# A pool mixer on rounded parts: three float32r products instead of one 32-bit product

## The chip, the cores and the metric

The kernel runs on one core of a Trainium2 chip. Times are device microseconds (us) of one launch. The median of three runs of the kernel before is 1588.48 us (1587.77 to 1590.91).

The core has five engines with a queue each: PE (TensorE, matrix products), DVE (VectorE), ACT (ScalarE), POOL (GpSimd) and SP (SyncE, which issues most DMA transfers). Each engine works through its queue in order, and waits on counters that other engines and transfers raise.

## The reference

Three layers over 512 tokens of 1024 features: a pool mixer with a feed-forward, latent attention with a feed-forward, differential attention with a routed mixture of 16 experts. Only the first step is changed, the pool mixer of layer 0 (its 1024 features are in four groups of 256, with windows of 2, 4, 8 and 16 tokens):

```python
def pool_mixer(h, w, scale):                 # h = rms_norm(x) * gain
    hf = h.reshape(B, S, 4, 256)
    cs = cumsum(hf, axis=1)
    for g, win in enumerate((2, 4, 8, 16)):
        c = cs[:, :, g]
        lag = pad(c[:, :-win], ((0, 0), (win, 0), (0, 0)))
        mean = (c - lag) / minimum(n_avail, win)[:, None]
        outs.append(mean - hf[:, :, g])      # a band matrix over tokens, less the identity
    y = einsum('bsgc,gcd->bsgd', stack(outs, axis=2), w)
    return y.reshape(B, S, D) * scale        # x = x + y
```

## The kernel before

The features lie on the 128 partitions, so x is eight tiles `x[:, d]` of 128 features by 512 tokens. `pool_mixer` computes the weight product first and the band after it, since both are linear and the norm's factor is one number per token:

1. `gains` (DVE): the group's weights `pw` times the norm's gain, two halves of 128x256.
2. `squares` (ACT, DVE): the square of each tile of x, added up on DVE; then `col_sums` (PE, a product with `ones` into the bank `pst`), `rcolv` (DVE) and the power -1/2 (POOL) give `rcol`, one factor per token.
3. `products` (PE): per group and pair of token tiles, x as the stationary operand against `pw`, into one PSUM bank; eight banks in all (four tagged `acc`, two `pss`, two `pst`). The products of groups 2 and 3 stand behind the column sums in PE's queue.
4. `evac`: each bank times `rcol` into a tile `z`, its first half by ACT and its second half by DVE.
5. the band products (PE): per feature tile, five products of `z` with the band matrix `bnd`, into an `acc` bank.
6. `finish`: DVE adds the scaled bank to x; ACT and DVE split the new x times the next gain into two float32r parts `xh` and `xl` (`xh` on ACT is the rounded value, `xl` on DVE the rest); ACT squares it and POOL adds the squares into `ss` for the norm of the feed-forward.

The products of `gains`, `products` and the bands are plain 32-bit ones; the profile shows each as two records. Everything later works on split operands: `mm3` makes three float32r products (high by high, high by low, low by high) of one.

Beside this the task `weights` starts the split of the feed-forward's first weights: a chunk `raw` of 128x2048 comes by DMA, ACT rounds a 128x512 part of it to `hi`, and DVE or POOL (parts 2 and 4) writes the rest to `lo`.

The order of instructions on each engine is fixed at build time. `Sched` interleaves the tasks: the ready task of the lowest rank goes next, and `Plan` keeps a rough line of time for each engine to say when a tile is ready. In this plan a chunk of weights counts as present. `gains` and `weights` have rank 0, `squares` and `evac` 1, `products` 2. All operations are issued in one wrapper, so the profile names them all L341. The feed-forward that follows needs all eight `xh` and `xl` in its first product, and the column sums of `ss` stand behind that product in PE's queue.

Of the kernel before, what the change touches and what calls it, by code (L numbers as in the profile page):

```python
# [17 lines left out]
P = 128  # L18
# [16 lines left out]
# the stream of the experts' weights: pieces in the arena while attending, routing, in the experts;  # L35
# pieces split ahead; chunks in the room of parts before the rows are gathered; chunks that come
# in pieces
# [4 lines left out]
# which parts of a chunk Pool takes the second halves of (feed-forward and first attention; second)  # L42
# [39 lines left out]
class Stream:  # L82
    """Weights in the order of their use: loaded ahead, split into two float32r parts ahead.
    Some are loaded into the arena, and the room of those that are not can take their parts.
    The experts' (from item `first` on) are split and used 512 columns at a time; they are
    loaded into the arena, up to `ahead` such pieces, or where parts had been."""
# [23 lines left out]
    def load(self):  # L110
        """as many of the coming ones as there is room for"""
# [59 lines left out]
    def open(self, t):  # L171
        """the first load after `hold`, and so all that follow, wait for the gathers before it"""
        if self.gate:
            self.net.nc.gpsimd.memset(t[:, :1], 0.0)
            self.gate = False

    def room(self):
        """the tags that the parts of the next one to split can have, if any are free"""
# [65 lines left out]
    def gone(self, i, last):  # L244
        """a part of item i is split"""
# [11 lines left out]
    def pump(self, n=1):  # L257
        """n more parts of the splits, as far as there is room"""
# [19 lines left out]
    def release(self, w=None):  # L278
        """the last use of w (or of the longest held) is issued"""
        i = 0 if w is None else [h is w for h, _ in self.held].index(True)  # L280
        for tag in self.held.pop(i)[1]:
            self.spare[tag] += 1
        if self.split >= self.first:
            self.load()
# [16 lines left out]
    def piece(self):  # L301
        """the next 512 columns of the experts' weights"""
# [7 lines left out]
class Plan:  # L310
    """What is issued, on each engine's line of time by a rough price list: when a tile will
    be there, so that a piece that needs it is issued no earlier."""
# [43 lines left out]
    def dma(self, price, *outs):  # L356
        """a transfer (into `outs`)"""
# [40 lines left out]
class Sched:  # L398
    """Interleaves tasks (generators) in program order. A task yields a tile that its next
    piece needs, or how long to wait; the first ready task of the lowest rank goes next."""  # L400
# [31 lines left out]
class Direct:  # L432
    """The weights of one expert whose number is known at run time only."""
# [20 lines left out]
class Net:  # L454
# [21 lines left out]
    def get(self, tag, n=1):  # L476
        """n PSUM banks, when as many are free"""
# [6 lines left out]
    def put(self, tag, n=1):  # L484
        """the last use of n banks is issued"""
# [18 lines left out]
    def hilo(self, hi, lo, src):  # L504
        """hi + lo = src"""
# [3 lines left out]
    def split(self, hi, lo, src, g=None):  # L509
        """hi + lo = src, or src * g, as a task"""  # L510
# [10 lines left out]
    def hilo_g(self, hi, lo, src, g):  # L521
        """hi + lo = src * g, g one number per partition"""
# [40 lines left out]
    def square_sum(self, key, src, first, scale=1.0, eng=None):  # L563
        """adds src^2 (one feature tile) to the sum of the norm"""
# [9 lines left out]
    def col_sums(self, key, ps=None):  # L574
        """sums of the squares per token, [token of the tile, tile], in PSUM"""
# [17 lines left out]
    def bcast(self, col, name, ps=None):  # L593
        """[token of the tile, tile] -> [every partition, token]"""
# [10 lines left out]
    def new_norm(self, gname, keep=False):  # L605
        """the parts of the coming norm's x; the ones in use stay with who holds the lists"""
# [4 lines left out]
    def prep(self, d, eng=None):  # L611
        """the split of x * gain, and the sum of squares, of feature tile d"""
# [4 lines left out]
    def norm_hooks(self):  # L617
        """what the first products of a phase leave to the tensor engine in between"""
# [8 lines left out]
    def pool_mixer(self):  # L627
        """tasks"""
        nc, a, sched = self.nc, self.a, self.sched
        self.ss = {}  # L630
        pw, bands, zs = [], [], {}
        for g in range(4):
# [7 lines left out]
        for g in range(4):  # L640
            b = self.tmp("bnd")
            nc.sync.dma_start(out=b[:, :384], in_=a["bands"][:, g])
            nc.dma(0.55, b)
            bands.append(b)
# [5 lines left out]
        def gains(g):  # L650
            yield pw[g]
            for k in range(2):
                c = slice(k * 256, (k + 1) * 256)
                nc.vector.tensor_scalar(pw[g][:, c], pw[g][:, c], self.vec("mix0", 2 * g + k),
                                        None, op0=OP.mult)

        def squares():
            for d in range(KT):
                yield self.x[:, d]
# [17 lines left out]
        def evac(g, jj, tag, ps):  # L677
# [3 lines left out]
            z = self.tmp("z")  # L681
            for j in range(2):
                o = slice(j * 256, (j + 1) * 256)
                r = self.rcol[:, 2 * jj + j:2 * jj + j + 1]
                if j:
# [1512 lines left out]
```

## Time and profile before

| what | value |
|---|---|
| median of three runs | 1588.48 us |
| span of the profiled execution, first to last instruction | 1588.0 us |
| own time of the profiled execution beside its span | not given; the median is 0.48 us above the span |
| PE busy | 1525.1 us, 96% |
| DVE, ACT, POOL busy | 1016.4, 773.0, 504.2 us |
| pool mixer, start to the first product of the feed-forward | 37.2 us |
| column sums of the feed-forward's norm on PE | from 44.73 us |

A row of the timeline gives the start, the time taken, the engine, and what is written from what; in brackets how long the engine sat idle before it and what ended the wait. Several equal instructions in a row are merged, with their count. A window's row gives its length, then the busy time (and count) of PE, PE's weight loads, DVE, ACT and POOL, PE's granted clock (1.00 is full speed, 2.4 GHz, and 0.50 is 1.2 GHz), the DMA engines' busy share and the GB/s moved. PE records are pipelined: the time from one start to the next is the price, not the length of one.

### The profile page before, as it was taken

To read this page: it belongs to the slowest core of one execution; us is meant where nothing else is said; L and a number is where in the kernel's file an instruction comes from. 1 tells how busy PE (TensorE), PEld (TensorE's weight loads), DVE (VectorE), ACT (ScalarE), POOL (GpSimd) and SP (SyncE) were. 2 spreads that over 40 slices of the span, in tenths; PEclk is the share of its full clock that TensorE was granted. 3 is DMA by queue.
4 is the path that set the end of the run, shared out by engine and by line. 5 is a ranking of instruction groups with operands and counts; after the bars stand their busy time and mean duration, and the time that the engine had idled before them with its cause. 6 is when DMAs were issued, how large, how long until landed. Compare 5 with 4: busy or idle time off the path is not lost. (4 is left out here: it accounts for less than half of the span.)

```text
span 1588.0 us, 21545 instructions
## 1 busy us (share of the span) xinstructions
PE 1525.1 (96%) x7752; PEld 1238.5 (78%) x7752; DVE 1016.4 (64%) x1668; ACT 773.0 (49%) x1569; POOL 504.2 (32%) x382
## 2 busy tenths in 40 slices
PE   7999999999999999999999999999999699999996
PEld 6788888888878788888888889889868566666664
DVE  5564344445477755443444467887884599999996
ACT  5323222323366633232223345566672378787875
POOL 3322122312241113221223123312221465565653
PEclk9999999999999999999999999999989699999998
DMA  6131323223210223213222232111067889999961
GB/s 237 61 106 55 118 106 106 89 74 103 83 44 29 65 107 119 98 58 123 106 107 71 84 124 81 54 54 67 27 205 260 243 305 357 371 350 352 341 209 29
DMA packets 69934, 221.60 MB, mean 140 GB/s; under 512 B 7616, under 2 KB 16960, under 8 KB 56640
## 3 DMA queue, kind: packets, MB, share of 16 engines
q1 hardware_dynamic: 56448, 201.03, 35.4%
q0 software_dynamic: 4064, 14.16, 3.8%
q10 hardware_dynamic: 9312, 5.01, 1.1%
q8 instruction: 62, 1.02, 0.3%
q14 instruction: 48, 0.39, 0.1%
HBM read 208.63 MB, written 11.53 MB: 139 GB/s over the span
## 5 line engine op out<-in xcount | busy, mean ns | idle before, releaser
L341 POOL TENSOR_TENSOR lo<-raw,hi 128x512 fp32r<-128x512 f32 (+1 forms) x157 | 224.4, 1440 | 714.1 <-ACT hi L341 625.8
L341 PE MATMUL acc<-xh,hi 128*128 128x512 f32 x744 | 290.5, 390 | 0.5 <-ACT xh L341 0.5
L341 PE MATMUL acc<-xl,hi 128*128 128x512 f32 x744 | 289.6, 389 | 0.3 <-DVE xl L341 0.3
L341 PE MATMUL acc<-xh,lo 128*128 128x512 f32 x744 | 289.5, 389 | 0.0
L341 DVE TENSOR_TENSOR wl<-raw,wh 128x512 fp32r<-128x512 f32 x288 | 264.8, 970 | 9.1 <-ACT wh L341 8.8
L341 ACT ACTIVATE hi<-raw 128x512 fp32r<-128x512 f32 (+1 forms) x378 | 208.7, 607 | 86.4 <-issue 59.8
L341 DVE TENSOR_TENSOR lo<-raw,hi 128x512 fp32r<-128x512 f32 (+1 forms) x221 | 211.7, 968 | 19.8 <-ACT hi L341 19.0
L341 ACT ACTIVATE wh<-raw 128x512 fp32r<-128x512 f32 x384 | 212.4, 621 | 16.2 <-PE acc L341 10.4
L341 POOL TENSOR_TENSOR wl<-raw,wh 128x512 fp32r<-128x512 f32 x96 | 143.3, 1493 | 123.8 <-ACT wh L341 88.8
L341 PEld LDWEIGHTS acc<-xh,hi 128*128 128x128 f32 x744 | 139.7, 188 | 29.6 <-ACT xh L341 1.0
L341 PEld LDWEIGHTS acc<-xl,hi 128*128 128x128 f32 x744 | 139.7, 188 | 29.3 <-DVE xl L341 0.6
L341 PEld LDWEIGHTS acc<-xh,lo 128*128 128x128 f32 x744 | 139.6, 188 | 29.1
L341 DVE TENSOR_TENSOR u<-acc,R 128x512 f32<-128x512 f32 x44 | 30.4, 691 | 181.1 <-PE acc L341 181.1
L341 PE MATMUL acc<-hh,hi 128*128 128x512 f32 x352 | 136.9, 389 | 0.0
L341 PE MATMUL acc<-hl,hi 128*128 128x512 f32 x352 | 136.9, 389 | 0.0
L341 PE MATMUL acc<-hh,lo 128*128 128x512 f32 x352 | 136.9, 389 | 0.0
L341 ACT ACTIVATE hh<-t 128x512 fp32r<-128x512 f32 x44 | 27.8, 632 | 218.4 <-DVE t L341 218.4
L341 DVE TENSOR_TENSOR x<-acc,x 128x512 f32<-128x512 f32 x59 | 40.5, 689 | 124.2 <-PE acc L341 124.2
L341 PE MATMUL acc<-hi,xh 128*128 128x256 f32 x384 | 112.7, 293 | 0.0
L341 PE MATMUL acc<-lo,xh 128*128 128x256 f32 x384 | 108.6, 283 | 0.0
L341 PE MATMUL acc<-hi,xl 128*128 128x256 f32 x384 | 108.5, 283 | 0.0
L341 PE MATMUL acc<-wh,teh 128*96 128x512 f32 x256 | 106.7, 417 | 0.0
(308 smaller groups left out, 2915.4 us busy)
## 6 DMA issues: line engine op xcount, KB each, us to landing
raw<-moe_w SPq DMA_DIRECT2D x200, 256.0 KB, 6.6
raw<-moe_w SPq DMA_DIRECT2D x46, 1024.0 KB, 8.4
raw<-ffn_gu SPq DMA_DIRECT2D x43, 1024.0 KB, 4.8
raw<-ffn_dn SPq DMA_DIRECT2D x32, 704.0 KB, 4.1
raw<-da_in SPq DMA_DIRECT2D x12, 1024.0 KB, 4.9
raw<-mla_up SPq DMA_DIRECT2D x4, 832.0 KB, 4.4
raw<-mla_o_a SPq DMA_DIRECT2D x12, 256.0 KB, 4.3
raw<-da_o_a SPq DMA_DIRECT2D x12, 256.0 KB, 4.2
```

What stands on the lines that cost most here:

```text
L341: r = f(*args, **kw)
```

## The change

x, the weights and z are split in two float32r parts, the weights' product becomes three products by `mm3`, and the bands become products of both parts of z with a rounded band. The band matrix is laid out anew on the host: four pieces of 128x512 whose first 128 columns are cut to their high bits, and a fifth piece with what the cut left; before it was four pieces of 128x384. New tasks are `parts` (rank 0: the split of x, high on ACT, low on DVE) and `rounded` (rank 0: POOL copies the bands to float32r). `gains` splits the weights, `evac` the bank: both halves on ACT (`zh`) and again on DVE (`zl`). `squares` now starts once a tile's parts are issued.

```diff
+        for g in range(5):
+            t = self.tmp("bndr")
+            nc.sync.dma_start(out=t, in_=a["bands"][:, g])
...
         def gains(g):
+            h = self.pair("pw")
             for k in range(2):
                 c = slice(k * 256, (k + 1) * 256)
-                nc.vector.tensor_scalar(pw[g][:, c], pw[g][:, c], self.vec("mix0", 2 * g + k),
-                                        None, op0=OP.mult)
+                self.hilo_g(h[0][:, c], h[1][:, c], pw[g][:, c], self.vec("mix0", 2 * g + k))
...
+        def rounded():
+            for t in raws:
+                yield t
+                b = self.tmp("bnd", F32R)
+                nc.gpsimd.tensor_copy(b, t)
+                yield b
+                bands.append(b)
+
+        def parts():
+            for d in range(KT):
+                yield self.x[:, d]
+                h = self.pair("xp")
+                self.hilo(*h, self.x[:, d])
+                xs[d] = h
 
         def squares():
             for d in range(KT):
-                yield self.x[:, d]
+                while xs[d] is None:
+                    yield 0.1
...
-                if j:
-                    nc.vector.tensor_scalar(z[:, o], ps[:, o], r, None, op0=OP.mult)
-                else:
-                    nc.scalar.activation(z[:, o], ps[:, o], AF.Copy, scale=r)
+                self.hilo_g(z[0][:, o], z[1][:, o], ps[:, o], r)
...
-                            self.mm(ps[:, (j % 2) * 256:(j % 2 + 1) * 256],
-                                    self.x[:, 2 * g + k, j * P:(j + 1) * P],
-                                    pw[g][:, k * 256:(k + 1) * 256], start=(k == 0),
-                                    stop=(k == 1))
+                            xh, xl = (t[:, j * P:(j + 1) * P] for t in xs[2 * g + k])
+                            wh, wl = (t[:, k * 256:(k + 1) * 256] for t in ws[g])
+                            self.mm3(ps[:, (j % 2) * 256:(j % 2 + 1) * 256], xh, xl, wh, wl,
+                                     k == 0, k == 1)
...
-                mm(0, b[:, 256:384], 0, 128, start=True)
-                mm(0, b[:, 128:256], 128, 256)
-                mm(2, b[:, 0:256], 256, 512)
-                mm(1, b[:, 0:256], 128, 384)
-                mm(3, b[:, 0:128], 384, 512, stop=True)
+                for n in range(2):
+                    mm(0, n, b[:, 0:256], 0, 256, start=(n == 0))
+                mm(0, 0, bands[4][:, g * P:(g + 1) * P], 0, 128)
+                for n in range(2):
+                    mm(2, n, b[:, 256:512], 256, 512)
+                for n in range(2):
+                    mm(1, n, b[:, 256:512], 128, 384)
+                for n in range(2):
+                    mm(3, n, b[:, 256:384], 384, 512, stop=(n == 1))
...
+        sched.spawn(parts(), 0)
+        sched.spawn(rounded(), 0)
```

From the first product of the feed-forward on, the instructions stand in the same order on every engine. In the mixer the order moves at three places. The first is ACT from the load of its table to the first evacuation, before (`sq` is a square of x, `hi` a rounded part of the feed-forward's weights):

```order
L341 ACT_TABLE_LOAD
L341 ACTIVATE sq<-x 128x512 x8
L341 ACTIVATE hi<-raw 128x512 x3
L341 ACTIVATE z<-pss,rcol 128x256
L341 ACTIVATE z<-acc,rcol 128x256 x4
```

And of the change, from the last split of x (`xph`) to the first evacuations:

```order
L341 ACTIVATE xph<-x 128x512 x2
L341 ACTIVATE hi<-raw 128x512
L341 ACTIVATE sq<-x 128x512
L341 ACTIVATE hi<-raw 128x512 x3
L341 ACTIVATE sq<-x 128x512
L341 ACTIVATE hi<-raw 128x512 x3
L341 ACTIVATE sq<-x 128x512
L341 ACTIVATE hi<-raw 128x512
L341 ACTIVATE sq<-x 128x512
L341 ACTIVATE zh<-pss,rcol 128x256 x4
```

The last four of the eight squares now stand behind rounded parts of two chunks of weights, where all eight stood ahead of them. The second place is ACT in the evacuation, with the counters that each instruction waits for, before:

```order
L341 ACTIVATE z<-pss,rcol 128x256 [waits PE_49,Pool_49]
L341 ACTIVATE z<-acc,rcol 128x256 x4
L341 ACTIVATE hi<-raw 128x512
L341 ACTIVATE z<-pss,rcol 128x256 [waits PE_49]
L341 ACTIVATE hi<-raw 128x512 [waits DMAHW2_49]
```

And of the change:

```order
L341 ACTIVATE zh<-pss,rcol 128x256 [waits PE_49,Pool_49]
L341 ACTIVATE zh<-pss,rcol 128x256 [waits DVE_49]
L341 ACTIVATE zh<-pss,rcol 128x256
L341 ACTIVATE zh<-pss,rcol 128x256 [waits DVE_49]
L341 ACTIVATE zh<-acc,rcol 128x256
```

The second half of each bank now waits on ACT for DVE's counter, and both banks `pss` go first. The third place is DVE from the norm's factor to the tail of the mixer, before:

```order
L341 TENSOR_SCALAR rcolv<-pst 128x4
L341 TENSOR_SCALAR z<-pss,rcol 128x256
L341 TENSOR_SCALAR z<-acc,rcol 128x256 x4
L341 TENSOR_TENSOR lo<-raw,hi 128x512
L341 TENSOR_SCALAR z<-pss,rcol 128x256
L341 TENSOR_SCALAR z<-pst,rcol 128x256
L341 TENSOR_TENSOR lo<-raw,hi 128x512
L341 TENSOR_SCALAR z<-pst,rcol 128x256
L341 SCALAR_TENSOR_TENSOR x<-acc,vecs,x 128x512
```

And of the change:

```order
L341 TENSOR_SCALAR rcolv<-pst 128x4
L341 SCALAR_TENSOR_TENSOR zl<-pss,rcol,zh 128x256 x4
L341 SCALAR_TENSOR_TENSOR zl<-acc,rcol,zh 128x256 x8
L341 SCALAR_TENSOR_TENSOR zl<-pst,rcol,zh 128x256 x4
L341 SCALAR_TENSOR_TENSOR x<-acc,vecs,x 128x512 x4
L341 SCALAR_TENSOR_TENSOR xl<-x,vecs,xh 128x512
```

Eight scalings of z on DVE become sixteen subtractions, and all of them stand ahead of the first sum into x.

## Rows read from the trace of the kernel before

**Rows 1.** The page's first line, and the window of one stretch of the feed-forward.

```profile
span 1588.0 us, 21545 instructions
...
100.00:300.00 200.00, 200.00 (x884) 165.62 (x883) 88.02 (x107) 55.73 (x103) 48.37 (x34) 1.00 0.28 98
```

**Rows 2.** Timeline of DVE, POOL and PE from the mixer's tail on.

```profile
28.48 0.73 DVE L341 SCALAR_TENSOR_TENSOR x<-acc,vecs,x 128x512 f32<-128x512 f32 x1
32.27 10.20 POOL L341 TENSOR_TENSOR ss<-ss,sq 128x512 f32<-128x512 f32 x6
38.49 2.82 DVE L341 SCALAR_TENSOR_TENSOR xl<-x,vecs,xh 128x512 fp32r<-128x512 f32 x2
42.77 0.75 DVE L341 SCALAR_TENSOR_TENSOR xl<-x,vecs,xh 128x512 fp32r<-128x512 f32 x1 [0.79 <-ACT xh L341]
43.39 1.28 POOL L341 TENSOR_TENSOR ss<-ss,sq 128x512 f32<-128x512 f32 x1 [0.93 <-ACT sq L341]
44.73 1.05 PE L341 MATMUL pst<-ones,ss 128*128 128x1 f32 x8 [0.43 <-POOL ss L341]
```

**Rows 3.** Timeline of PE in the mixer: start, time, engine, operation.

```profile
6.88 8.66 PE L341 MATMUL acc<-pw,x 128*128 128x256 f32 x32 [6.88 <-DMA x<-xT]
16.98 1.02 PE L341 MATMUL pst<-ones,sq 128*128 128x1 f32 x8 [1.45 <-DVE sq L341]
17.87 3.70 PE L341 MATMUL pss<-pw,x 128*128 128x256 f32 x16
24.95 12.53 PE L341 MATMUL acc<-bnd,z 128*128 128x128 f32 x80
```

**Rows 4.** Timeline of ACT and of SP's issues, 13 to 24 us.

```profile
13.68 1.15 ACT L341 ACTIVATE sq<-x 128x512 f32<-128x512 f32 x2 [0.77 <-DMA x<-xT]
14.15 18.51 SPq L124 DMA_DIRECT2D raw<-ffn_gu  x5
19.77 1.67 ACT L341 ACTIVATE hi<-raw 128x512 fp32r<-128x512 f32 x3 [4.95 <-DMA raw<-ffn_gu]
23.32 0.47 ACT L341 ACTIVATE z<-pss,rcol 128x256 f32<-128x256 f32 x1 [1.88 <-POOL rcol L341]
```

**Rows 5.** Windows of two microseconds while the first weights arrive (columns as in rows 1).

```profile
14.00:16.00 2.00, 1.53 (x8) 1.00 (x6) 1.79 (x3) 0.83 (x2) 0.00 (x0) 1.00 0.72 175
20.00:22.00 2.00, 2.00 (x11) 1.77 (x10) 0.76 (x2) 1.44 (x3) 0.99 (x1) 1.00 1.04 430
```

**Rows 6.** Windows of one microsecond around a stretch where PE waits, late in the kernel.

```profile
1240.00:1241.00 1.00, 0.00 (x0) 0.00 (x0) 0.65 (x2) 0.57 (x1) 1.00 (x2) 0.50 1.00 346
1257.00:1258.00 1.00, 1.00 (x5) 0.95 (x6) 0.00 (x0) 0.09 (x1) 0.00 (x0) 0.50 1.02 383
1263.00:1264.00 1.00, 1.00 (x6) 0.65 (x5) 0.46 (x4) 0.98 (x3) 0.63 (x1) 1.00 0.57 217
```

**Rows 7.** Timeline of PE, float32r products of 256 columns in the second attention.

```profile
960.10 0.28 PE L341 MATMUL acc<-hi,xh 128*128 128x256 f32 x1
960.22 0.28 PE L341 MATMUL acc<-hi,xl 128*128 128x256 f32 x1
```

**Rows 8.** Timeline of DVE and POOL, the norm's factor and a cast on POOL.

```profile
21.05 0.15 DVE L341 TENSOR_SCALAR rcolv<-pst 128x4 f32<-128x4 f32 x1
22.23 1.05 POOL L341 TENSOR_TENSOR rcol<-rcolv,mhalf 128x4 f32<-128x4 f32 x1
59.38 0.28 POOL L341 CAST mask_b<-causal 128x128 bf16<-128x128 f32 x1
```

**Rows 9.** Timeline of ACT and DVE in the evacuation of the banks.

```profile
23.69 1.57 ACT L341 ACTIVATE z<-acc,rcol 128x256 f32<-128x256 f32 x4
24.23 1.65 DVE L341 TENSOR_SCALAR z<-acc,rcol 128x256 f32<-128x256 f32 x4
26.52 0.51 ACT L341 ACTIVATE z<-pst,rcol 128x256 f32<-128x256 f32 x1
27.06 0.48 DVE L341 TENSOR_SCALAR z<-pst,rcol 128x256 f32<-128x256 f32 x1 [0.19 <-ACT z L341]
```

More of the change, by code (lines that the diff above doesn't have):

```diff
@@ L631, in pool_mixer @@
         pw, bands, zs = [], [], {}
+        xs, ws, raws = [None] * KT, [None] * 4, []
         for g in range(4):
@@ L639, in pool_mixer @@
             nc.dma(1.46, self.x[:, 2 * g], self.x[:, 2 * g + 1])
[L640 to L644, printed above, removed]
+        for g in range(5):
+            t = self.tmp("bndr")
+            nc.sync.dma_start(out=t, in_=a["bands"][:, g])
+            nc.dma(0.73, t)
+            raws.append(t)
         self.constants()
@@ L651, in gains @@
             yield pw[g]
+            h = self.pair("pw")
             for k in range(2):
                 c = slice(k * 256, (k + 1) * 256)
-                nc.vector.tensor_scalar(pw[g][:, c], pw[g][:, c], self.vec("mix0", 2 * g + k),
-                                        None, op0=OP.mult)
+                self.hilo_g(h[0][:, c], h[1][:, c], pw[g][:, c], self.vec("mix0", 2 * g + k))
+            yield h
+            ws[g] = h
+        def rounded():
[11 more added lines that the diff above has]
+                xs[d] = h
         def squares():
             for d in range(KT):
-                yield self.x[:, d]
+                while xs[d] is None:
+                    yield 0.1
                 q = self.tmp("sq")
@@ L680, in evac @@
             yield ps
-            z = self.tmp("z")
+            z = self.pair("z")
             for j in range(2):
@@ L708, in products @@
                     ps = yield from self.get(tag)
-                    yield pw[g], self.x[:, 2 * g], self.x[:, 2 * g + 1]
+                    while ws[g] is None or xs[2 * g + 1] is None:
+                        yield 0.1
+                    yield xs[2 * g] + xs[2 * g + 1]
                     for j in (2 * jj, 2 * jj + 1):
                         for k in range(2):
-                            self.mm(ps[:, (j % 2) * 256:(j % 2 + 1) * 256],
-                                    self.x[:, 2 * g + k, j * P:(j + 1) * P],
-                                    pw[g][:, k * 256:(k + 1) * 256], start=(k == 0),
-                                    stop=(k == 1))
+                            xh, xl = (t[:, j * P:(j + 1) * P] for t in xs[2 * g + k])
+                            wh, wl = (t[:, k * 256:(k + 1) * 256] for t in ws[g])
+                            self.mm3(ps[:, (j % 2) * 256:(j % 2 + 1) * 256], xh, xl, wh, wl,
+                                     k == 0, k == 1)
                     sched.spawn(evac(g, jj, tag, ps), 1, ps)
@@ L721, in products, with mm @@
                     yield 0.1
+                while len(bands) < 5:
+                    yield 0.1
                 ps = yield from self.get("acc")
-                yield bands[g]
-                def mm(j, rhs, c0, c1, start=False, stop=False):
+                yield tuple(bands)
+                def mm(j, n, rhs, c0, c1, start=False, stop=False):
                     o = (j % 2) * 256 + hd * P
-                    self.mm(ps[:, c0:c1], zs[g, j // 2][:, o:o + P], rhs, start, stop)
+                    self.mm(ps[:, c0:c1], zs[g, j // 2][n][:, o:o + P], rhs, start, stop)
                 b = bands[g]
-                mm(0, b[:, 256:384], 0, 128, start=True)
-                mm(0, b[:, 128:256], 128, 256)
-                mm(2, b[:, 0:256], 256, 512)
-                mm(1, b[:, 0:256], 128, 384)
-                mm(3, b[:, 0:128], 384, 512, stop=True)
+                for n in range(2):
[7 more added lines that the diff above has]
+                    mm(3, n, b[:, 256:384], 384, 512, stop=(n == 1))
                 sched.spawn(finish(d, ps), 1, ps)
@@ L2149, in _host @@
     o["ident"] = np.eye(P, dtype=np.float32)
-    b = np.zeros((P, 4, 384), np.float32)
+    b = np.zeros((P, 5, 512), np.float32)
     p, c = np.arange(P)[:, None], np.arange(256)[None, :]
+    first = []
     for g, w in enumerate(WINDOWS):
         inside = (c - p >= 0) & (c - p < w)
-        b[:, g, :256] = inside * np.float32(1.0 / w) - (c == p)
+        b[:, g, 256:] = inside * np.float32(1.0 / w) - (c == p)
         n = np.minimum(c[:, :P] + 1, w).astype(np.float32)
-        b[:, g, 256:] = inside[:, :P] / n - (c == p)[:, :P]
+        first.append(inside[:, :P] / n - (c == p)[:, :P])
+        b[:, g, 128:256] = b[:, g, 384:]
+    first = np.stack(first, axis=1).astype(np.float32)
+    high = (first.view(np.uint32) & np.uint32(0xFFFFE000)).view(np.float32)
+    b[:, :4, :P] = high
+    b[:, 4] = (first - high).reshape(P, 4 * P)
     o["bands"] = b
```

## The prediction

> **What bounds the kernel now.** I read first the page's span and the windows by stage, then the timeline of the first 50 us by engine, since only the mixer at the very start changes. The reader is to see two things in the windows. The whole is 1588.0 us, and behind the mixer PE is the bound: 200.00 us busy of 200 from 100 to 300 us [rows 1]. Nothing there waits for a time of day; weights are loaded when earlier ones have been used. So whatever the mixer loses or wins passes to the end, and I take the shift of one instruction, the column sums `pst<-ones,ss` of the feed-forward's norm at 44.73 us [rows 2], as the shift of the whole.
>
> In the timeline of PE the mixer looks bound by PE: products of groups 0 and 1 to 15.54, column sums at 16.98, then groups 2 and 3, and bands without a gap from 24.95 to 37.48 [rows 3]. But PE is bound only in the middle. The evacuation waits until 23.32 for the norm's factor [rows 4], and from 28.48 on DVE writes x and `xl` back to back while POOL adds squares; the column sums wait for POOL's last add [rows 2]. Three stretches set the end: the way to the factor, the evacuation, the tail on DVE and POOL.
>
> **The way to the factor.** Before, all eight squares of x are done by 14.83 on ACT, and only then does ACT wait for the first chunk of weights, until 19.77 [rows 4]. The change puts the last four squares behind seven, or for the last eight, rounded parts of two chunks (the first fence of ACT's order). The column sums, and in PE's queue behind them the products of groups 2 and 3, now wait for the weights from memory.
>
> The first chunk lands at 19.7 before, 5.6 us after its issue at 14.15 [rows 4]. Now 0.5 MB more of bands stands ahead of it (five pieces of 256 KB for four of 192 KB). At 430 GB/s [rows 5] that is 1.2 us; but the slice from 14 to 16 us moved only 175 GB/s and has room. I take 1.0 us: 20.7, between 20.0 and 21.5. From there ACT issues twelve instructions of 128x512 up to the last square, one each 0.53 us (three take 1.67, two 1.15 [rows 4]): the last ends at 20.7 + 11 x 0.53 + 0.6 = 27.1. The work that the change adds on ACT and DVE ahead of this, the splits of x and of the weights, fits in the wait: before, ACT is idle for 4.95 us there [rows 4]. A last add on DVE, 0.7 to 1.1 beside POOL's subtraction, gives 28.2 for the column sums instead of 16.98.
>
> PE has then been idle since about 15 us. The trace has such a case: with PE waiting at 1240 the granted clock is 0.50, still 0.50 when PE is full again at 1257, and 1.00 in the window at 1263 [rows 6]. That is under 6 us at half speed; I take three quarters of it, and price PE's return at 1.2 GHz for its first 4.5 us: column sums 2.0 (twice the 1.02 [rows 3]), then 12 products at 0.213 (256 columns at 1.2 GHz), and the other 12 of the two `pss` banks at 0.12 (960.10 to 960.22 [rows 7]): 28.2 + 2.0 + 2.55 + 1.44 = 34.2. The factor itself is earlier: 0.15 on DVE and 1.05 on POOL [rows 8] behind the column sums, about 31.6. POOL's cast of a band ahead of it is 128x512, which no row shows; four times a cast of 128x128 is 1.1 us [rows 8], a subtraction of its size 1.28 [rows 2], and it ends while PE is at its sums. The evacuation starts at 34.2 instead of 23.32: **+10.9**. Bounds: 31.0 (chunk at 20.0, clock never down) and 35.5 (half clock through both banks).
>
> **The evacuation.** Before, ACT and DVE each take half of eight banks, and DVE's x follows 5.2 us after the start (23.32 [rows 4] to 28.48 [rows 2]). Now each engine passes over both halves, and the second fence of ACT's order shows that the second half waits for DVE. So a bank is a chain: ACT high, DVE low, ACT high, DVE low. An ACT half is 0.49 (0.47 [rows 4], 0.51 [rows 9]), a hand-over 0.03 (DVE's z at 27.06 behind ACT's end at 27.03 [rows 9]). DVE's `zl` of 128x256 is not in the trace: between a scaling of that size, 0.48 [rows 9], and the two-tensor form at twice the size, 0.73 [rows 2]. I take 0.50, near the row of its size. The next bank's first half on ACT overlaps DVE's second, so from bank to bank it is 0.50 + 0.03 + 0.49 + 0.03 + 0.41 (DVE's start to start, four in 1.65 [rows 9]) = 1.46. Eight banks to the first x: 0.52 + 7 x 1.46 + 1.05 + 0.41 = 12.2, against 5.2: **+7.0**. With 0.73 it is 4 us more; without the wait it would be 0.52 + 16 x 0.41 = 7.1.
>
> A row shows that wait already: the DVE half of a bank sat idle 0.19 us until ACT's half ended [rows 9]; there the two also share the output tile. The Trainium skill, "PSUM — Partial Sum Buffer", section "PSUM bank collisions raise a hardware error", says that no two engines may touch one bank (in the same partitions) at once, reads included. By that rule the alternation holds for reads alone and the stretch is 12.2; by a reading of the row as a shared tile it is 7.1. The trace agrees with the rule as far as it goes.
>
> **The tail.** From the first x to the column sums it takes 16.25 us before (28.48 to 44.73 [rows 2]). The same eight x, eight `xl` and seven adds remain. Four x now stand first, so the first square reaches POOL after some 4.5 us instead of 3.8; then five adds at 1.70 (six in 10.20) and two at 1.28 [rows 2] give 15.6. The last four `xl` stand in a row, though, and two in a row beside POOL's adds took 2.82 where one alone takes 0.75 [rows 2]; paced so, the last `xl` and with it PE's product come at about 16.5. I take 16.2: **0**. The bands have 9 products of 0.12 per tile, 1.1 us, at half clock 1.9, and DVE needs one each 1.7: covered.
>
> The Trainium skill, "SBUF — State Buffer", section "Who interferes with whom", has a DVE instruction with two inputs from there and a POOL instruction that reads there exclude each other for a whole instruction. By it, adds and `xl` alternate and 16.5 is the better figure; by the adds' own pace it is 15.6. The pair at 2.82 agrees with the rule.
>
> **Sum.** 10.9 + 7.0 + 0 = +17.9 us on the profiled execution, 1605.9 for its span. The median of the runs is 0.48 us above that span, so 1606 for the time. What PE saves (bands 12.53 [rows 3] to 8 x 1.1 = 8.8; groups 2 and 3 to 5.8) is not on this path and is priced at nothing; it is hidden by the waits for DVE.
>
> **The rivals.**
> - *A lighter chain.* The halves are evacuated at DVE's own pace (7.1 instead of 12.2, +12.8 in all), or PE's clock stays up (start at 31.9, +15.6), or both (+10.5): 1599 to 1604. For it: the clock reads 1.00 in all windows of the mixer before. Against: there PE never sat idle for over ten microseconds once it had begun.
> - *A heavier one.* The clock falls again while PE waits through the evacuation and the feed-forward begins at half speed: its first 24 products of 512 columns take 24 x 2 x 0.213 = 10.2 us instead of 24 x 2 x 0.12 = 5.8, and with bands at 1.9 a tile the column sums come 3 to 5 us later; or `zl` is near 0.73: 1609 to 1613. For it: in rows 6 the clock stayed down for over 5 us of full work. Against: PE's product is paced by `xl` anyway.
> - *Faster.* PE is the bound throughout, as its timeline suggests, and its saving shows: 3.7 in the bands and 1.4 in groups 2 and 3, 5 us less, 1583. That decides if the evacuation starts no later than 23.3 and lasts no longer than before. Even with the weights present the moment ACT is free (about 16.8) the squares end at 23.2, so I see no way to it but a wrong reading of the order.
> - *No change.* The experts at the end stream weights; if the loads gained there all that the start lost, the time would stay 1588. Their loads follow buffers that PE frees, against it.
>
> **How the numbers follow.** Forecast, +15 to +21: 0.58. Lighter, +8 to +15: 0.22. Heavier, +21 to +27: 0.13. No change: 0.04. Faster: 0.03. A difference of 0.2%, 3.2 us, is about what a measurement can tell from none. Slower by more is 0.93, within 0.04, faster 0.03. The range from 1598 (the lighter case with both) to 1612 (the upper bound of the start and part of a dearer `zl`) leaves out some 2 in 10.
>
> **What would show it.** In the profile after: ACT waits near 20.7 for `raw`, with squares behind it; PE idles from about 15 to 28 ahead of `pst<-ones,sq`, and the granted clock reads 0.50 behind that; ACT's `zh` starts near 34 and every second one waits for DVE; the first x on DVE is near 46 and `pst<-ones,ss` near 62. Wrong if the squares end before the weights land, if `zh` runs without waits, or if `pst<-ones,ss` lies within 3 us of 44.7.

## The result, and the profile after

The changed kernel takes 1610.05 us (median of four runs, 1607.32 to 1611.75) beside 1589.7 for the kernel before (the three runs above and a fourth): over all these runs 1.0119 times as long, with a 95% interval of 1.0085 to 1.0154, and 1.0128 by the two medians, so 19 to 20 us slower. The forecast was 1606, between 1598 and 1612. The profiled execution has a span of 1609.4 us and a time of 1611.22; its span is 21.4 above the one before.

Behind the mixer nothing is changed but the time of day: PE is again full from 100 to 300 us.

```profile
100.00:300.00 200.00, 200.00 (x884) 165.62 (x883) 93.00 (x111) 55.73 (x103) 49.02 (x34) 1.00 0.28 98
```

**The way to the factor.** The timeline of ACT shows the weights arriving at 18.87, and the last four squares between the splits of `raw`, the last one done at 24.60 + 0.61 = 25.21. [rows 4] had all eight done by 14.83.

```profile
18.87 0.63 ACT L341 ACTIVATE hi<-raw 128x512 fp32r<-128x512 f32 x1 [3.36 <-DMA raw<-ffn_gu]
...
23.56 0.61 ACT L341 ACTIVATE sq<-x 128x512 f32<-128x512 f32 x1
24.08 0.61 ACT L341 ACTIVATE hi<-raw 128x512 fp32r<-128x512 f32 x1
24.60 0.61 ACT L341 ACTIVATE sq<-x 128x512 f32<-128x512 f32 x1
36.93 0.48 ACT L341 ACTIVATE zh<-pss,rcol 128x256 fp32r<-128x256 f32 x1 [11.72 <-PE pss L341]
```

But ACT is not the last. DVE works through the same mixture of squares and weights, and from 23.37 to 28.39 us each of its instructions takes some 1.75 us, where one alone takes 0.6 to 0.7. POOL's subtractions beside them take 1.68 each:

```profile
21.09 1.34 DVE L341 TENSOR_TENSOR lo<-raw,hi 128x512 fp32r<-128x512 f32 x1 [0.87 <-ACT hi L341]
22.36 1.09 DVE L341 TENSOR_TENSOR sq<-sq 128x512 f32<-128x512 f32 x1
23.37 1.75 DVE L341 TENSOR_TENSOR lo<-raw,hi 128x512 fp32r<-128x512 f32 x1
25.05 1.75 DVE L341 TENSOR_TENSOR sq<-sq 128x512 f32<-128x512 f32 x1
26.72 1.74 DVE L341 TENSOR_TENSOR lo<-raw,hi 128x512 fp32r<-128x512 f32 x1
28.39 1.89 DVE L341 TENSOR_TENSOR sq<-sq 128x512 f32<-128x512 f32 x2
...
22.87 5.05 POOL L341 TENSOR_TENSOR lo<-raw,hi 128x512 fp32r<-128x512 f32 x3
```

So PE's column sums start at 30.42 (16.98 in [rows 3]), after 14.87 us without work, and at half speed: the sums take 1.84 instead of 1.02, and the first 17 products of group 2 follow each other by 0.21 (0.12 behind them). The windows, with the granted clock as the third number from the end, show when it fell and when it came back:

```profile
30.42 1.84 PE L341 MATMUL pst<-ones,sq 128*128 128x1 f32 x8 [14.87 <-DVE sq L341]
32.48 0.41 PE L341 MATMUL pss<-pwl,xph 128*128 128x256 f32 x1
32.69 0.41 PE L341 MATMUL pss<-pwh,xpl 128*128 128x256 f32 x1
...
16.00:18.00 2.00, 0.00 (x0) 0.00 (x0) 2.00 (x4) 0.00 (x0) 0.00 (x0) 1.00 1.03 431
18.00:20.00 2.00, 0.00 (x0) 0.00 (x0) 0.64 (x2) 1.13 (x3) 0.00 (x0) 0.67 1.00 422
20.00:22.00 2.00, 0.00 (x0) 0.00 (x0) 1.13 (x2) 2.00 (x5) 1.39 (x2) 0.50 1.02 430
34.00:36.00 2.00, 2.00 (x12) 2.00 (x12) 0.00 (x0) 0.00 (x0) 0.23 (x1) 0.56 0.00 0
36.00:38.00 2.00, 2.00 (x19) 2.00 (x19) 0.48 (x1) 0.52 (x2) 0.00 (x0) 1.00 0.03 8
66.00:68.00 2.00, 2.00 (x10) 1.71 (x10) 0.16 (x1) 0.00 (x0) 1.02 (x1) 0.62 0.04 8
68.00:70.00 2.00, 2.00 (x7) 1.58 (x6) 0.00 (x0) 0.00 (x0) 0.00 (x0) 0.53 0.00 0
```

**The evacuation and the tail.** On DVE, `zl` takes 0.48 and every second one waits some 0.55 for ACT; from one such pair to the next it is 1.42 (41.30 to 42.72). The first x is at 48.80 (28.48 in [rows 2]). In the tail the last four `xl` stand in a row beside POOL's additions, 1.7 each:

```profile
41.30 0.88 DVE L341 SCALAR_TENSOR_TENSOR zl<-acc,rcol,zh 128x256 fp32r<-128x256 f32 x2 [0.55 <-ACT zh L341]
42.72 0.88 DVE L341 SCALAR_TENSOR_TENSOR zl<-acc,rcol,zh 128x256 fp32r<-128x256 f32 x2 [0.55 <-ACT zh L341]
48.80 2.72 DVE L341 SCALAR_TENSOR_TENSOR x<-acc,vecs,x 128x512 f32<-128x512 f32 x4
58.16 6.87 DVE L341 SCALAR_TENSOR_TENSOR xl<-x,vecs,xh 128x512 fp32r<-128x512 f32 x4
...
53.32 11.16 POOL L341 TENSOR_TENSOR ss<-ss,sq 128x512 f32<-128x512 f32 x7 [19.09 <-ACT sq L341]
65.08 0.50 PE L341 MATMUL acc<-xl,hi 128*128 128x512 f32 x1 [0.72 <-DVE xl L341]
65.66 0.95 PE L341 MATMUL pst<-ones,ss 128*128 128x1 f32 x8
```

The column sums of the feed-forward's norm come at 65.66 instead of 44.73 [rows 2]: +20.9.

**A better mark for comparisons.** Single times of one kernel lie up to 13 us apart here, and the experts' stage at the end adds or takes a few us of its own (in the profile of weights_only, below, POOL's last `rcol` ahead of the experts is 16.0 later than before, 1255.22 for 1239.26, and the span 11.3 longer). I therefore compare the runs by a mark in the middle too: POOL's `rcol` of the next norm, in the attention layer, at 405.05 before and 427.47 after, +22.4. These are the two rows, of before first:

```profile
405.05 1.48 POOL L341 TENSOR_TENSOR rcol<-rcolv,mhalf 128x4 f32<-128x4 f32 x1
```

```profile
427.47 1.49 POOL L341 TENSOR_TENSOR rcol<-rcolv,mhalf 128x4 f32<-128x4 f32 x1
```

From the feed-forward's factor (POOL's `rcol` again, before and after) to this mark it is 358.99 before and 360.58 after:

```profile
46.06 1.03 POOL L341 TENSOR_TENSOR rcol<-rcolv,mhalf 128x4 f32<-128x4 f32 x1 [1.39 <-DVE rcolv L341]
```

```profile
66.89 1.02 POOL L341 TENSOR_TENSOR rcol<-rcolv,mhalf 128x4 f32<-128x4 f32 x1 [2.41 <-DVE rcolv L341]
```

The 1.6 us fit the stretch at 0.62 and 0.53 of the clock from 66 to 70 in the windows above (2 x 0.38 + 2 x 0.47 = 1.7 us of lost clock, an estimate). In the three kernels below whose windows read 1.00 behind the tail (two_banks, bands_only, first_and_two_banks) it takes 358.96 to 358.99, as before.

### The profile page after: what moved, and what is told of

Its sections match the earlier page's. It is cut to its first block, busy times and chain, and to the rows that moved or that the text cites. A ratio compares the mean times of both kernels' runs of the same rounds, so it can differ in the third digit from the quotient of the medians.

```text
span 1609.4 us, 21647 instructions
## 1 busy us (share of the span) xinstructions
PE 1525.1 (95%) x7776; PEld 1240.7 (77%) x7776; DVE 1035.1 (64%) x1684; ACT 783.5 (49%) x1593; POOL 506.6 (31%) x387
## 3 DMA queue, kind: packets, MB, share of 16 engines
q8 instruction: 62, 1.02, 0.2%
```

## The experiments

Ten kernels, each timed beside the kernel before (whose medians were 1589.0 to 1590.5 there; the ratios are to these, over all runs). "Sums", "z", "x" and "ss" are the starts in the profile of the first norm's column sums, the first evacuation on ACT, the first x on DVE, and the feed-forward's column sums; "factor" is that norm's `rcol`; "layer 1" is the mark above.

| kernel | median us | ratio [95%] | sums | z | x | ss | factor | layer 1 |
|---|---|---|---|---|---|---|---|---|
| before | 1588.48 (three runs) | 1 | 16.98 | 23.32 | 28.48 | 44.73 | 46.06 | 405.05 |
| after | 1610.05 | 1.0119 [1.0085, 1.0154] | 30.42 | 36.93 | 48.80 | 65.66 | 66.89 | 427.47 |
| squares_first | 1602.11 | 1.008 [1.0059, 1.0102] | 23.69 | 26.96 | 40.52 | 57.60 | 58.83 | 419.37 |
| two_banks | 1605.21 | 1.0098 [1.0079, 1.0116] | 30.41 | 35.12 | 44.26 | 60.62 | 61.95 | 420.94 |
| no_pool_lo | 1605.27 | 1.01 [1.008, 1.0121] | 27.61 | 30.88 | 42.75 | 59.57 | 60.80 | 420.88 |
| warm | 1609.39 | 1.0127 [1.0104, 1.015] | 30.32 | 34.42 | 46.29 | 64.19 | 66.17 | 426.72 |
| bands_only | 1602.47 | 1.0068 [1.0048, 1.0087] | 16.65 | 23.46 | 38.10 | 54.95 | 56.18 | 415.16 |
| weights_only | 1606.9 | 1.0099 [1.0072, 1.0126] | 29.39 | 32.66 | 40.99 | 59.52 | 60.99 | 421.43 |
| first_and_two_banks | 1598.32 | 1.0041 [1.0024, 1.0058] | 24.52 | 27.79 | 37.15 | 53.80 | 55.03 | 413.99 |
| before_sums_on_pe | 1597.48 | 1.0047 [1.0031, 1.0063] | 16.00 | 22.59 | 27.75 | none | 45.13 | 411.17 |
| before_factor_first | 1590.01 | 1.0004 [0.9994, 1.0014] | 16.50 | 19.46 | 26.11 | 44.52 | 46.67 | 407.96 |
| after_best | 1600.18 | 1.0058 [1.0041, 1.0075] | spread | 28.07 | 37.94 | 55.22 | 56.45 | 415.42 |

**The squares ahead of the weights again** (squares_first).

```diff
         def weights():
-            yield 14.0
+            while self.rcol is None:
+                yield 0.1
```

> The changed kernel, but the first parts of the feed-forward's weights are split only after the column sums of the first norm are issued; so on ACT the last four squares stand ahead of the splits of raw, as in the kernel before. Nothing else of the change is undone. Theory (some 13.6 of the 21 us are the squares' wait for the weights from memory, and the clock that PE loses meanwhile): the column sums of the norm start near 18 to 20 us instead of 30.4, the evacuation near 21.5 to 24 instead of 36.9, the granted clock does not fall to 0.50 ahead of it; the evacuation itself stays as long (11 to 12 us) and takes some 2 us more for subtractions that now stand in it; the end comes 10 to 13 us earlier than in the changed kernel, 1597 to 1600 us. Rival (the chain of the evacuation and the tail carry nearly all, the squares hide behind PE's products): less than 4 us, 1606 or more.

The direction holds, the size falls short: ss and layer 1 are 8.1 us earlier, not 10 to 13, and the time 1602.11. The column sums come at 23.69, not 18 to 20, and the clock fell all the same. DVE is the reason: its queue holds the splits of x and of the mixer's weights ahead of the additions, and works without a gap from 13.55 to the last addition, part of it slowed by POOL's casts of the bands (an addition at 16.07 takes 1.09 beside them, 0.68 alone).

```profile
17.09 1.69 DVE L341 TENSOR_TENSOR xpl<-x,xph 128x512 fp32r<-128x512 f32 x2
18.70 4.84 DVE L341 TENSOR_TENSOR sq<-sq 128x512 f32<-128x512 f32 x5
```

So of the 13.4 us by which the sums are late, 6.7 come from the order of squares and weights, and 6.7 stay with the order undone: the change's own work on DVE, with POOL's casts beside it. The evacuation starts 10 us earlier, not 6.7, because it also takes the banks of groups 0 and 1 first, which wait for the factor alone. It then takes 13.56 to the first x instead of 11.87, since two subtractions of the feed-forward's weights now stand in it.

**Neighbours of different banks** (two_banks).

```diff
             for j in range(2):
                 o = slice(j * 256, (j + 1) * 256)
-                r = self.rcol[:, 2 * jj + j:2 * jj + j + 1]
-                self.hilo_g(z[0][:, o], z[1][:, o], ps[:, o], r)
...
+                for jj in range(2):
+                    r = self.rcol[:, 2 * jj + j:2 * jj + j + 1]
+                    self.hilo_g(z[jj][0][:, o], z[jj][1][:, o], pss[jj][:, o], r)
```

> The changed kernel, but the evacuation takes the two banks of a group together: ACT writes zh of bank A half 0, bank B half 0, A half 1, B half 1, and DVE its zl in the same order, so that neighbours on ACT are of different banks. Theory (the second half on ACT waits for DVE on the same bank, 1.42 us from bank to bank): waits between zh and zl go, the stretch from the first zh to the first x falls from 11.9 to 16 x 0.5 + 0.5 = 8 to 8.5 us, the end 3 to 4 us earlier, 1606 to 1607. Rival (ACT and DVE wait for each other whatever the bank, by their start-up or by what they read and write): the stretch stays at 11 us or more and the time at 1610.

The waits on ACT fall from 0.58 at every second `zh` to 0.2 at every fourth, and eight banks pass with the pace of the two engines:

```profile
38.29 0.83 ACT L341 ACTIVATE zh<-acc,rcol 128x256 fp32r<-128x256 f32 x2
39.34 1.59 ACT L341 ACTIVATE zh<-acc,rcol 128x256 fp32r<-128x256 f32 x4 [0.21 <-DVE zl L341]
41.15 0.87 ACT L341 ACTIVATE zh<-acc,rcol 128x256 fp32r<-128x256 f32 x2 [0.21 <-DVE zl L341]
```

x comes 4.5 us earlier, ss 5.0, layer 1 6.5; the last 1.5 because the clock reads 1.00 behind its tail. The evacuation starts 1.8 earlier, with PE's first bank `pss` ready and not the second, and so its 9.14 us, over the 8 to 8.5 forecast, have 1.30 in them for the second bank from PE.

In this run neighbours differ in the bank and in the tiles `zh` and `zl` as well, so it does not tell by itself which of the two ACT waits for. The split of the mixer's weights in the changed kernel does. It goes through the same helper, with the same two halves of one pair of tiles, only that it reads SBUF and no bank; ACT's second half runs on there, until 6.87, while DVE works on the first from 6.50:

```profile
5.96 0.91 ACT L341 ACTIVATE pwh<-pw,vecs 128x256 fp32r<-128x256 f32 x2
6.50 0.89 DVE L341 SCALAR_TENSOR_TENSOR pwl<-pw,vecs,pwh 128x256 fp32r<-128x256 f32 x2 [6.50 <-ACT pwh L341]
```

So the shared tiles are not the reason. The chain belongs to the order of the two engines' passes over one bank.

**POOL out of DVE's way** (no_pool_lo).

```diff
-        if self.part in POOLED[self.phase]:
+        if self.part in POOLED[self.phase] and i >= 2:
             self.flush(nc.gpsimd)
```

> The changed kernel, but the subtractions of the first two chunks of weights that POOL took (four of 128x512) are on DVE. Theory (DVE's adds of squares ran 1.75 us each because they and POOL's subtractions shut each other out): with more work on DVE its subtractions and adds still take 0.7 to 0.9 us each, and the norm's column sums start earlier, near 28 us instead of 30.4. The scheduler then also evacuates the banks of groups 0 and 1 ahead of groups 2's, so that the evacuation begins with the factor, near 31 to 32 us; the end 3 to 5 us earlier, 1605 to 1607. Rival (DVE's instructions are slow for another reason, or the adds wait for ACT's squares): they stay at 1.7 us, the three more put the column sums at 31 us or later, and the end stays at 1610.

The theory holds, to 0.4 us: DVE has three subtractions more ahead of the sums, and these start 2.8 us earlier, with 0.6 to 0.7 us an instruction where it had 1.7. z and x come 6.05 earlier; the other 3.2 are the banks of groups 0 and 1 standing first, as in squares_first:

```profile
22.36 0.69 DVE L341 TENSOR_TENSOR sq<-sq 128x512 f32<-128x512 f32 x1
22.96 1.89 DVE L341 TENSOR_TENSOR lo<-raw,hi 128x512 fp32r<-128x512 f32 x3
24.77 0.68 DVE L341 TENSOR_TENSOR sq<-sq 128x512 f32<-128x512 f32 x1
25.37 0.68 DVE L341 TENSOR_TENSOR lo<-raw,hi 128x512 fp32r<-128x512 f32 x1
```

The Trainium skill ("SBUF — State Buffer", section "Who interferes with whom") says that a DVE instruction with two inputs from there and a POOL instruction that reads there shut each other out. By that rule a pair takes one instruction of each, 0.6 and 1.28 (POOL's addition of that size at 43.39 in [rows 2]), some 1.9; measured is 1.68 from one to the next on both engines. The two traces agree that they take turns, and to 0.2 us with that price.

**PE kept at work** (warm). 64 products of no use stand between group 1 and the column sums.

```diff
...
+                        for n in range(64):
+                            nc.nc.tensor.matmul(wps, xs[3][0][:, :P], xs[3][0], start=True,
+                                                stop=True)
...
```

> The changed kernel, and PE multiplies 64 times 128x128 by 128x512 of float32r into a bank that nobody reads, between the products of group 1 and the norm's column sums, where it sat idle from 15.5 to 30.4 us. Theory (the clock fell because PE had nothing to do, and costs 1 us in the column sums, some 2 in the products of group 2 and 3, and in the bands nothing that DVE does not hide): the granted clock stays at 1.00 until 30 us, column sums take 1.0 instead of 1.84, the 24 products of group 2 2.9 instead of 4.8, the evacuation starts 2 to 3 us earlier, the end comes 2 to 3 us earlier, 1607 to 1608. Rival (the clock is without weight, since the factor or DVE sets the pace): within 1 us of 1610.

In the mixer the theory holds: the clock stays at 1.00 to 40 us, the sums take 1.02, the evacuation starts 4.10 behind them instead of 6.51, so the half clock cost 2.4 us there. But the gain does not last. The clock falls again in the evacuation, at the end of the tail it reads 0.50 where the changed kernel had 1.00, ss is only 1.5 us earlier, layer 1 0.75, and the time is 1609.39, no different from the changed kernel's. That is the rival's number but not its reason: the clock had weight, and cost at the tail most of what it gave ahead of it.

```profile
62.00:64.00 2.00, 1.97 (x5) 1.06 (x4) 1.12 (x1) 0.00 (x0) 0.57 (x1) 0.50 0.00 0
64.00:66.00 2.00, 2.00 (x10) 1.90 (x10) 0.07 (x1) 0.00 (x0) 0.00 (x0) 0.50 0.00 0
```

**Each part alone** (bands_only, weights_only). The first is the kernel before with the new `rounded`, `evac` and bands; the second the changed kernel with the old `evac`, bands and their layout.

> One part of the change alone: the kernel before, with z split in two, bands rounded by POOL's casts and two products of float32r per band; the weights' products stay plain 32-bit ones, and x is not split. Theory (the evacuation's chain and the tail belong to this part, the late column sums to the other): the squares stand ahead of the weights' splits as in the kernel before, column sums near 17 us, the evacuation starts at 23.3 to 24.5, takes 12 to 13 us to the first x (two or three of the weights' subtractions stand in it), and from there 16.5 to 17 us to the column sums of the feed-forward's norm: 52.5 to 54.5 instead of 44.73, +8 to +10 us, 1598 to 1600. Rival (the parts are not separable: the evacuation is slow only behind a cold PE): +2 us or less, 1592.

bands_only: z at 23.46, first x 14.64 us later, 16.85 to ss. The tail is as forecast; the way to x is 2 us more than 12 to 13, since two `lo` of the weights stand ahead of the first x at 2.37 beside POOL. ss +10.2, layer 1 +10.1, 1602.47, a little over the range. The evacuation's chain needs no cold PE.

```profile
35.81 2.37 DVE L341 TENSOR_TENSOR lo<-raw,hi 128x512 fp32r<-128x512 f32 x2
```

> The other part alone: x and weights split in two and three products for the weights, but z stays in one piece of 32 bits, evacuated half by ACT and half by DVE, and the bands are plain 32-bit products without casts. Theory: column sums near 30 us, PE at half clock behind them, the evacuation begins with the factor near 33 us with the banks of group 0 and takes 5 to 7 us to the first x, the tail 16 to 17: column sums of the feed-forward's norm at 55 to 58 instead of 44.73, +11 to +13 us, 1601 to 1603; with the bands' part that makes 20 to 22, the whole change. Rival (the parts hide each other): the two sum to less than 15 or more than 27 us.

weights_only: ss +14.8, layer 1 +16.4, 1606.9, more than the +11 to +13 forecast. The first x comes 8.33 behind z, not 5 to 7, since ACT waits 2.35 for PE's `pss`. From x to ss it takes 18.5, not 16 to 17: PE's plain bands set the pace of the first x (idle 0.54 and 0.78 behind PE's `acc` in DVE's rows). The two parts sum to 26.5 at layer 1, against 22.4 for both, and to 28.4 by the medians, against 20.4. So they do hide some 4 us of each other, at the edge of what the rival named (27), which is not out. At ss 2.3 of the 4.1 lie in the tail, where the whole change does not wait for bands; the rest lies ahead of the first x, and no run takes it apart.

```profile
40.99 0.75 DVE L341 SCALAR_TENSOR_TENSOR x<-acc,vecs,x 128x512 f32<-128x512 f32 x1 [0.54 <-PE acc L341]
42.52 0.75 DVE L341 SCALAR_TENSOR_TENSOR x<-acc,vecs,x 128x512 f32<-128x512 f32 x1 [0.78 <-PE acc L341]
```

**Both edits on the changed kernel** (first_and_two_banks).

> The changed kernel with both edits: the weights' splits only behind the first norm's column sums, and the evacuation with two banks of a group in turn. Theory (they act on stretches that follow each other): the evacuation starts at 27 as in the run with the first edit alone, takes 9 to 10 us instead of 13.6, the column sums of the feed-forward's norm come at 53 to 54.5 instead of 57.6, 3 to 4.5 us less: 1597 to 1599. Rival (with a faster evacuation the products of group 3, at half clock to 31 us and done at 33.7, become the wait): 56 us or later, 1600 or more.

z 27.79, x 37.15, ss 53.80, layer 1 at +8.9, 1598.32: the effects nearly add (8.1 and 5.0 at ss alone, 11.9 together), and 11.7 us of the change's loss are order alone.

**Two tries at the kernel before.** before_sums_on_pe drops POOL's additions and lets PE sum each square:

```diff
-            self.square_sum("x", self.x[:, d], "x" not in self.ss, eng=nc.gpsimd)
+            q = self.tmp("sq")
+            nc.scalar.activation(q, self.x[:, d], AF.Square)
+            sqs[d] = q
...
+                for j in range(NT):
+                    self.mm(ps[:, j:j + 1], sqs[d][:, j * P:(j + 1) * P], self.ones,
+                            start=(d == 0 and j == 0), stop=(d == KT - 1 and j == NT - 1))
```

> The kernel before, with one edit in the tail: the squares for the feed-forward's norm are not added up on POOL; PE takes the column sums of each of the eight square tiles into one bank (32 small products instead of 4). Theory (in the tail POOL's additions and DVE's subtractions shut each other out, which sets 1.7 us a step): without POOL's additions DVE's x and xl take 0.66 each back to back, the last xl comes 3 to 4.5 us earlier, and so does the factor of that norm: 1585 to 1587. Rival (PE's 28 more small products, some 0.25 us each, stand ahead of bands and products and take back what DVE wins): within 1.5 us of the kernel before, or slower.

The theory missed: +7 us, on the rival's side ("or slower"). The small products do hold up the bands (DVE waits 1.01, 0.78 and 1.02 for PE's `acc`), and the last `xl` comes no earlier than before. The factor is 0.9 earlier, but my edit put the feed-forward's first product behind all the sums, which the rival did not name. PE begins it at 44.72, where the kernel before began it at 37.23; its 24 products are then still ahead, some 5.5 us at 0.23 each, and part of them at half clock.

```profile
43.80 1.05 PE L341 MATMUL pst<-ones,sq 128*128 128x1 f32 x8 [0.44 <-ACT sq L341]
44.72 0.48 PE L341 MATMUL acc<-xh,hi 128*128 128x512 f32 x1
```

before_factor_first starts the weights' splits only when the factor is there, and issues one chunk's:

```diff
-            yield 14.0
-            for i in range(8):
+            while not self.rcol:
+                yield 0.1
+            for i in range(4):
```

> The kernel before with the order lesson applied to it: in its trace DVE's first instruction of the norm's factor (21.05 us) stands behind a subtraction of the weights that waits for them from memory, though the column sums end near 18.0. Here the weights' splits begin only when the factor is there, and only the first chunk's four are issued in the mixer. Theory: the factor is ready near 19.4 instead of 23.3, the first x comes at 26.6 to 27 instead of 28.48 (PE's bands bound it then), and the tail loses the POOL subtraction ahead of its additions: column sums of the feed-forward's norm at 42 to 43 instead of 44.73; 2 to 3 us faster than the kernel before, 1587 to 1588.5. Rival (PE is the bound from 17 to 37 us, and the tail keeps its own pace): less than 1 us.

The factor is 4.3 us earlier (POOL's `rcol` at 17.88 instead of 22.23), the first x 2.4, and ss 0.2: the rival. From x on the tail has its own pace, PE's bands and the pairs of `xl` and additions. Behind it the clock falls (0.59 and 0.50 in the windows): the column sums take 1.87 instead of 1.05, and layer 1 is even 2.9 later; the time is that of the kernel before.

**All on the changed kernel** (after_best): both edits, one chunk, and each square of the first norm summed by PE.

```diff
-                if d == 0:
-                    self.ss["x"] = q
-                else:
-                    yield q
-                    nc.vector.tensor_tensor(self.ss["x"], self.ss["x"], q, op=OP.add)
+                yield q
+                for j in range(NT):
+                    self.mm(ps[:, j:j + 1], q[:, j * P:(j + 1) * P], self.ones,
+                            start=(d == 0 and j == 0), stop=(d == KT - 1 and j == NT - 1))
```

> The changed kernel with all that the runs point to: the weights' splits behind the factor and of the first chunk only, the evacuation over two banks in turn, and the column sums of the first norm taken by PE from each of the eight squares (32 small products instead of 4), so that DVE's seven additions, queued behind its splits of x, are gone. Theory: sums complete near 22.5 to 23.5, evacuation from 24 to 25 us, first x at 33 to 34.5, column sums of the feed-forward's norm at 50 to 51.5 instead of 65.66; the clock does not fall before the evacuation; 1594.5 to 1597, still 4 to 7 us behind the kernel before, since the evacuation has twice the passes and the tail its own pace. Rival (DVE's queue of splits is what holds the evacuation): no earlier than 27 us, and 1598 as with the two edits alone.

A miss: z at 28.07, 1600.18. The number is the rival's, the cause is not: DVE sat idle 9.62 us for PE. ACT's squares were all done by 17.52, but PE only begins the last five squares' sums at 21.15, and they take 5.48 us, at a falling clock. PE is late because it starts slowly: up to 17.59 its products follow each other by 0.21 (10.55 to 10.76), half the pace of 0.12 behind that, although the window from 10 to 12 reads 1.00. At full pace the stretch from 8.49 to 17.59 would be up to 4.5 us shorter (an estimate, half of it); the sums end 3 to 4 us later than the theory had them.

```profile
10.55 0.41 PE L341 MATMUL acc<-pwl,xph 128*128 128x256 f32 x1
10.76 0.41 PE L341 MATMUL acc<-pwh,xpl 128*128 128x256 f32 x1
21.15 5.48 PE L341 MATMUL pst<-ones,sq 128*128 128x1 f32 x40
...
10.00:12.00 2.00, 2.00 (x10) 2.00 (x11) 1.78 (x4) 2.00 (x6) 0.00 (x0) 1.00 1.04 384
22.00:24.00 2.00, 2.00 (x20) 2.00 (x20) 0.00 (x0) 0.00 (x0) 0.00 (x0) 1.00 0.84 348
24.00:26.00 2.00, 2.00 (x13) 2.00 (x13) 0.00 (x0) 0.00 (x0) 0.00 (x0) 0.62 0.00 0
26.00:28.00 2.00, 2.00 (x10) 2.00 (x11) 0.16 (x1) 0.00 (x0) 1.01 (x1) 0.50 0.00 0
...
26.67 0.16 DVE L341 TENSOR_SCALAR rcolv<-pst 128x4 f32<-128x4 f32 x1 [9.62 <-PE pst L341]
```

No version beats the kernel before.

## Why the prediction was right, and where its steps were off

The direction, the three stretches and two of the three prices held; the way to the factor was under-priced by 2.7 us. The forecast of +15 to +21 holds by the medians (+20.4), but not by the span of the profile (+21.4) or beside the 1588.48 that it started from (+21.6); these lie in what the prediction called a heavier chain. So it held by a narrow margin.

1. *The way to the factor: +10.9 forecast, +13.6 measured (23.32 to 36.93), above the stated bound of 35.5.* The order on ACT was read rightly, and the weights landed earlier than forecast (18.87, not 20.7; the last square ended at 25.21, not 27.1). The term that failed is "a last add on DVE, 0.7 to 1.1 beside POOL's subtraction". The additions stand in DVE's queue between subtractions of weights, and from 23.37 on they alternate with POOL's at 1.75; the last ends at 30.3. From the last square to the sums it took 5.2 us, not 1.1. That the total is off by less is luck: the 1.9 us by which the weights came early hid part of these 4.1. I had used this very exclusion for the tail and not for this queue. no_pool_lo shows what it costs: 2.8 us.
2. *"The work that the change adds on ACT and DVE ... fits in the wait".* True of the changed kernel, where the squares are later still. squares_first shows that it hides only there: once the squares are early, DVE's splits hold the sums at 23.7.
3. *PE's clock.* Forecast 6.0 us from the sums to the evacuation, measured 6.51: half speed lasted to about 35.8, through 17 of 24 products instead of 12. warm prices it: 4.10 without. The lighter rival ("PE's clock stays up") is out. The case of [rows 6] was no pure wait, though: from 1238 to 1240, before PE stood idle, the windows read 0.87 and 0.50 with PE busy 1.00 and 0.94, on products of 1 and of 128 columns.
4. *The evacuation: +7.0 forecast, +6.7 measured* (11.87 from the first zh to the first x). The bank-to-bank price of 1.46 was 1.42, `zl` 0.48 where 0.50 was taken. two_banks shows that the wait, not the passes, makes about 4 us of it (2.7 in the stretch, and the 1.30 that it spends on PE's second bank). That puts out the other half of the lighter rival.
5. *The tail: 0 forecast, +0.6 measured* (16.86 instead of 16.25), by the pace of `xl`, 16.5 by the rule beside it.
6. *Behind the column sums.* Nothing was priced there; the clock at 0.62 and 0.53 adds 1.6. It is a small form of the rival "a heavier one".

In sum +13.6 + 6.7 + 0.6 = +20.9 at the column sums, 22.4 at layer 1, 21.4 in the span and 20.4 between the medians. What PE saves showed nowhere, as priced: it is hidden by DVE; of the versions of the change, weights_only is the one where the bands' saving is missed.

Some figures of the prediction were loose without moving its sum. Of the last four squares only two stand behind seven and eight rounded parts, the other two behind one and four. The 1.28 called a subtraction [rows 2] is an addition. With PE's clock up the start comes to 32.1, not 31.9. ACT was free at 15.51, not about 16.8. At half clock a tile's bands, 1.9, are not covered by the 1.7 of DVE: in warm DVE waits 0.52 for one.

Open: why the clock falls behind some tails and not behind others (two_banks, bands_only and first_and_two_banks keep 1.00 there), and how the end of the kernel evens out some us: before_factor_first is 2.9 later at layer 1, 1.3 at POOL's last `rcol` ahead of the experts (1240.52 for 1239.26), and level at the end.

## What to carry to other kernels

Cheaper products won nothing here, where two other engines prepare the operands: count the passes over each tile on ACT and DVE first, then what stands ahead of the one value that everything waits for. When a change adds work to a queue, price every instruction ahead of the awaited one at the pace it has beside its neighbour engine, not alone. Where two engines pass over one PSUM bank in turn, let them alternate between two banks; here that took some 4 us off the evacuation.

## What the runs showed of the hardware

- 128x512 additions and subtractions on DVE took 0.6 to 0.7 us alone and 1.75 beside POOL's subtractions, which took 1.68 each: giving POOL's to DVE made the sums behind them start 2.8 us earlier.
- The granted clock fell to 0.62 and 0.50 in windows in which PE was busy throughout (after_best, 24 to 28 us), behind and during products of one column.
- At the start of a run the clock's column did not show PE's pace: in after_best float32r products of 256 columns followed each other by 0.21 until 17.59 and by 0.12 behind it, while the windows read 1.00.
- ACT and DVE passing in turn over both halves of a PSUM bank took 1.42 us a bank; alternating between two banks they took 0.9 (four banks of `acc` from 38.29 to 41.91 in two_banks).
- A few us at half clock behind the column sums of the feed-forward's norm cost 1.5 to 2.3 us up to layer 1 (358.99 between the two factors before, 360.58 after, 361.29 in before_factor_first). In warm the clock read 0.50 ahead of these sums too, and 1.8 of the 2.5 us gained at the first x were gone at the factor.
